# Moving the pools of small tiles so that large tiles begin at multiples of 64 bytes, in a hybrid GLA, retention and mixture-of-experts block

## The chip, the cores and the metric

The kernel runs on one core of one Trainium2 chip. The metric is the device time of the whole program in microseconds (us). Three runs of the kernel before gave 2324.79, 2324.49 and 2323.91 us; the median is 2324.49 us.

## What is computed

One decoder block over 1,024 tokens of width 1,024, all in float32. Cut to what matters:

```python
def reference(x, ...):
    u = _rmsnorm(x, norm_mix_w)
    proj = u @ w_in                               # 1024 x 11280: q, k, v, gates of two mixers
    o_gla = _gla_chunked(...)                     # 4 heads, gated linear attention
    o_ret = _retention_chunked(...)               # 4 heads, rotary, per-head decay
    y_a, y_b = o_gla @ w_branch_gla, o_ret @ w_branch_ret
    h = x + (sigmoid(mga) * y_a + sigmoid(mgb) * y_b) @ w_out
    t = _rmsnorm(h, norm_ffn_w)
    # router: best of 4 groups, then the 2 best of its 8 experts; 32 experts in all
    for each expert e, for the tokens that chose it:
        hid = silu(t @ wg[e]) * (t @ wu[e])       # 1024 -> 512
        ffn += weight * (hid @ wd[e])             # 512 -> 1024
    return _rmsnorm(h + ffn, norm_final_w)
```

## The kernel before, in words

**Products.** Nearly all of the arithmetic is done by one line, L153, in `Acc.add`. Each operand is split into two float32r parts, hi = the rounded value and lo = the rest (`split`, L136 to L143: ScalarE writes hi, VectorE writes lo), and a product is three matmuls into one PSUM bank: hi with hi, hi with lo, lo with hi. A matmul has a stationary operand (128 or 112 columns, loaded into the array) and a moving one (512 columns, that is 2,048 bytes of every partition). In the rows below the moving operand stands first behind the arrow: `bank<-w_hi,uh` moves `w_hi` over a stationary `uh`.

**First part, the mixers.** Two halves of 512 tokens. Weights come in slabs of 1 MB (`load_w`, L156): the SP queue loads `w_raw`, `split` makes `w_hi` and `w_lo`, one slab ahead of its use. Four kinds of products use them: `feat` (L320) has the weights stationary and moves `uh`/`ul`; `toks` (L328) has `uh`/`ul` stationary and moves the weights; `gla_y` and `ret_y` (L569, L761) have the weights stationary and move tiles of the pool `slots`; `project` (L806) has tiles of `slots` stationary and moves the weights. A fifth kind, in `ret_scores`, `ret_state` and `ret_out` (L650, L692, L721), has both operands in `slots`. The order of all steps is written out by hand in `prog` (L996 to L1127).

**Second part, the experts.** 32 experts, up to CAP = 112 rows each (L1173 to L1252). The rows are gathered by POOL's queue into `xg`, turned and split into `xh`/`xl` (L1184), which are the stationary operands of the gate and up products: eight blocks of 112 columns each, 448 bytes apart. The hidden layer is turned and split into `hh`/`hl` (L1230), four such blocks, stationary in the down products. The moving operands are the weights, `m_hi`/`m_lo`, split from `m_raw`: 6 slabs of 1 MB for each expert, 190 of them through whole raw buffers. A raw buffer (L1152) is one of eleven, used in turn: four of `upool`, two of `wraw`, five of `mraw`; for the last 58 slabs only the first six are used. The SP queue issues a slab's load as soon as VectorE has finished reading the buffer (L1199).

**Where tiles lie.** Pools are placed one behind the other in each partition in the order in which they are opened, and every tile takes a multiple of 32 bytes. `consts` begins at byte 16,512 and ends at 41,632. The memory map of the kernel before is then, by adding up the tiles:

| pool (opened in this order) | its large tiles | begins at byte | past a multiple of 64 |
|---|---|---|---|
| wraw | w_raw, m_raw | 41,632 | 32 |
| wsp | w_hi, w_lo, m_hi, m_lo | 58,016 | 32 |
| small (4,672 bytes) | none | 90,784 | 32 |
| ypool | yb, hid, hh, hl | 95,456 | 32 |
| rsm (3,680 bytes) | none | 111,840 | 32 |
| upool | uh, ul, m_raw | 115,520 | 0 |
| trig, slots (mixers) | slot | 148,288; 152,384 | 0 |
| mp, mk, mraw (experts, in the place of trig and slots) | xh, xl; xg; m_raw | 148,288; 163,264; 188,160 | 0 |

Of the kernel before, what the change touches and what calls it, by code (L numbers as in the profile page):

```python
# [18 lines left out]
F32 = mybir.dt.float32  # L19
F32R = mybir.dt.float32r  # L20
BF16 = mybir.dt.bfloat16
I32 = mybir.dt.int32
# [21 lines left out]
NEARLY = 2  # L44

# layout of the packed table of constants (columns)
# [9 lines left out]
def _const_table():  # L56
    """Constants that follow from the shapes alone."""
# [26 lines left out]
# 2*pi in three parts, the first two short enough for exact products  # L84
# [4 lines left out]
def hybrid_block(tc, a, out, dbg=None):  # L89
# [25 lines left out]
    psum = top.enter_context(tc.tile_pool(name="psum", bufs=8, space=bass.MemoryType.PSUM))  # L115
    wraw = top.enter_context(tc.tile_pool(name="wraw", bufs=2))
    wsp = top.enter_context(tc.tile_pool(name="wsp", bufs=2))
    small = top.enter_context(tc.tile_pool(name="small", bufs=2))
# [5 lines left out]
    def rsqrt(dst, src, n, p=128):  # L124
        """dst = 1/sqrt(src): a guess from the bits, then Newton's steps."""
        t = small.tile([128, 16], I32, name="rs_i", tag="rs_i")[:p, :n]
        y = small.tile([128, 16], F32, name="rs_y", tag="rs_y")[:p, :n]
        b = small.tile([128, 16], F32, name="rs_b", tag="rs_b")[:p, :n]
        DVE.tensor_scalar(t, src.bitcast(I32), 1, None, op0=OP.logical_shift_right)  # L129
        DVE.tensor_scalar(y.bitcast(I32), t, -1, 0x5f3759df, op0=OP.mult, op1=OP.add)  # L130
        for i in range(3):
            DVE.tensor_mul(b, y, y)  # L132
            DVE.scalar_tensor_tensor(b, b, -0.5, src, op0=OP.mult, op1=OP.mult)  # L133
            DVE.scalar_tensor_tensor(dst if i == 2 else y, b, 1.5, y, op0=OP.add, op1=OP.mult)

    def split(hi, lo, src, scale=None):  # L136
        """src (times scale per partition) = hi + lo, both with 12 significant bits."""
# [7 lines left out]
    class Acc:  # L145
        """Products of split operands summed in one bank."""
# [9 lines left out]
    def load_w(src, kt, n, swap=False):  # L156
        """A slab of weights [128, kt, n], split; swap: even columns first, then odd ones."""
# [18 lines left out]
    rsm = top.enter_context(tc.tile_pool(name="rsm", bufs=1))  # L176
# [3 lines left out]
    slots = mixers.enter_context(tc.tile_pool(name="slots", bufs=NSLOT))  # L180

# [48 lines left out]
    # kept across the halves  # L230
# [3 lines left out]
    # per assignment, for products with one-hots: its row in two parts, its weight in three  # L234
# [9 lines left out]
    junk = consts.tile([128, 512], BF16, name="junk")  # L244
# [5 lines left out]
    def sq_sum(dst, src, cols):  # L250
        """dst = sum of squares of src along its free axis."""
# [3 lines left out]
    def rms_tail(rstd, s2, n, p=128):  # L255
        """rstd[:, :n] = 1 / rms of n tiles' rows, from the squares of their column halves."""
# [5 lines left out]
    class Half:  # L262
        """One half of the sequence on its way through the mixers."""
# [16 lines left out]
        def norm_x(self, t):  # L280
            """The rows of one tile, scaled."""
# [19 lines left out]
        def start_x(self):  # L301
            """Tile after tile, as they come."""
# [17 lines left out]
        def feat(self, w, c0):  # L320
            """Features [c0, c0+128) of the slab w, for all tokens of the half: [128 features, 512]."""
# [6 lines left out]
        def toks(self, w, part, accs):  # L328
            """Rows 512*part.. of a [1024, 512] block of weights: adds to [128 tokens, 512] for each tile."""
# [24 lines left out]
        def decay_a(self):  # L354
            """log sigmoid(z) = min(z, 0) - ln(1 + exp(-|z|))"""
# [12 lines left out]
        def decay_b(self):  # L368
            self.mn = small.tile([128, 4], F32, name="mn")
# [8 lines left out]
        def decay_c(self):  # L378
            self.ep, self.en = [], []
            self.el = small.tile([128, 4, 4], F32, name="el")  # L380
# [8 lines left out]
            mn1 = small.tile([128, 1], F32, name="mn1")  # L389
# [3 lines left out]
        def decay_d(self):  # L393
            ps = bank()
            PE.transpose(ps[0:1, 0:128], self.mn1, ident)
            mn2 = small.tile([1, 2], F32, name="mn2")
# [60 lines left out]
        def gla_chunk(self, c, pair):  # L457
# [7 lines left out]
            for j in range(2):  # L465
# [5 lines left out]
                if not last:  # L471
# [5 lines left out]
                    else:  # L477
                        tmp = small.tile([128, 256], F32, name="s_tmp", tag="s_tmp")
# [4 lines left out]
        def gla_exact(self):  # L483
            """Where a chunk's decay leaves float32's range: the recurrence itself, one column of the
            state after the other, along the tokens."""
            half = self.half
            flag = nc.values_load(flag_i[0:1, half:half + 1], min_val=0, max_val=1)
            with tc.If(flag > 0):  # L488
                ones = small.tile([128, 1], F32, name="ones_f")
# [14 lines left out]
                for h in range(4):  # L504
# [10 lines left out]
                    with tc.For_i(0, 256, n) as i:  # L515
                        s0 = small.tile([128, n], F32, name="s0")
# [4 lines left out]
                        s1 = small.tile([128, n], F32, name="s1")  # L521
# [10 lines left out]
                        ob = small.tile([128, 4, n], F32, name="ob")  # L532
# [36 lines left out]
        def gla_y(self, w, c):  # L569
            """y_a, gated: features 256c.."""  # L570
# [46 lines left out]
        def rotary(self, w):  # L617
            """The slab's 256 features, rotated: raw and split, even ones then odd ones."""
# [31 lines left out]
        def ret_scores(self):  # L650
            """Scores, transposed, causal."""
            self.ph, self.pl = [], []
            for j in range(4):
# [11 lines left out]
                dg = small.tile([128, 128], F32, name="diag", tag="diag")  # L665
# [48 lines left out]
        def ret_hand(self):  # L714
            """What the rest of the head's work takes, kept apart from the next head's."""
# [5 lines left out]
        def ret_out(self, h):  # L721
            o = self.o
            mv = small.tile([128, 4, 2], F32, name="mv")
            for i in range(4):
# [10 lines left out]
                bs = small.tile([128, 6], F32, name="bs", tag="bs")  # L735
# [3 lines left out]
            # rstd of the decayed rows, with the decay: g^i / sqrt(g^2i var + eps)  # L739
# [101 lines left out]
        def route_a(self):  # L841
            """The rows that the experts gather."""
# [9 lines left out]
        def route_b(self):  # L852
# [11 lines left out]
            def first_max(src, n, name):  # L864
                """Its maximum along the last axis and the one-hot of the first place that has it."""
# [34 lines left out]
        def route_c(self):  # L900
            """Each assignment's place among its expert's rows."""
# [16 lines left out]
        def route_d(self):  # L918
            """The weights, in three parts of 8 bits for the products with one-hots."""
# [87 lines left out]
    def seq(z):  # L1007
        """Lists of steps of one half, by name."""
# [62 lines left out]
    def middle(half, mix):  # L1071
        """From the gated branch to the last head's projections; mix: steps put between, by place."""
# [70 lines left out]
    # =========================================================================  # L1143
# [1 line left out]
    moe = contextlib.ExitStack()  # L1145
    mp = moe.enter_context(tc.tile_pool(name="mp", bufs=2))
    mk = moe.enter_context(tc.tile_pool(name="mk", bufs=1))
    mraw = moe.enter_context(tc.tile_pool(name="mraw", bufs=NRAW))
# [24 lines left out]
    class Expert:  # L1173
        """One block of up to CAP rows of one expert."""
# [9 lines left out]
        def rows(self):  # L1184
            self.xh = mp.tile([128, 8, CAP], F32R, name="xh")
            self.xl = mp.tile([128, 8, CAP], F32R, name="xl")
# [27 lines left out]
        def room(self):  # L1214
            """For the hidden layer: rows, and turned in two parts."""
# [14 lines left out]
        def turn(self):  # L1230
# [4 lines left out]
            self.hh, self.hl = (z[:, :4 * CAP].rearrange("p (k t) -> p k t", k=4) for z in (self.hh, self.hl))  # L1235
# [26 lines left out]
    class Spill(Expert):  # L1262
        """The same with buffers that no load running ahead waits for, and the Pool's queue."""
# [4 lines left out]
        def room(self):  # L1268
            return [self.xg[:, :512], mp.tile([128, 8, CAP], F32R, name="hh", tag="xh").rearrange("p k t -> p (k t)"),
                    mp.tile([128, 8, CAP], F32R, name="hl", tag="xl").rearrange("p k t -> p (k t)")]  # L1270

    def overflow(xg):
        """The rows past the first CAP of an expert, a block of CAP at a time."""
        cf = mk.tile([1, 32], F32, name="cf")
        ci = mk.tile([1, 32], I32, name="ci")
        nb_f = mk.tile([1, 1], F32, name="nb_f")
        nb_i = mk.tile([1, 1], I32, name="nb_i")
# [5 lines left out]
        with tc.If(nb > 0):  # L1283
            gix2 = mp.tile([CAP, 32], I32, name="gix2")
            swt2 = mp.tile([CAP, 32], F32, name="swt2")
            with tc.For_i(0, nb, 1):
# [12 lines left out]
                with tc.For_i(0, NEXP, 1) as e:  # L1299
                    left = nc.values_load(ci[0:1, ds(e, 1)], min_val=0, max_val=SEQ)  # L1300
                    with tc.If(left > 0):
                        gi = mp.tile([CAP, 1], I32, name="gi")
                        wi = mp.tile([CAP, 1], F32, name="wi")
# [11 lines left out]
    # the down products of one come after the gate and up products of the next, save at a pause  # L1315
    pauses = (2, NEXP - 2, NEXP - 1)
    firsts = [mraw.tile([128, 2048], F32, name="m_raw", tag="m_raw") for i in range(NRAW)]
    for z in firsts[NEARLY:]:
        # the first rows come before these loads
# [83 lines left out]
```

## Time and profile before

| | |
|---|---|
| runs (three) | 2323.91 to 2324.79 us, median 2324.49 us |
| span of the profiled execution | 2320.6 us, from its first instruction to its last (3.9 us below the median of the runs; the page gives no other time of that execution) |
| busy, share of that span | PE 95%, weight loads 76%, VectorE 57%, ScalarE 47%, POOL 6% |
[...]
| DMA | 406 MB, 175 GB/s over the span |

How to read it: the mixers take the first two thirds of the span, with PE busy nearly throughout and the DMA engines about a third busy. After a thin stretch (end of the mixers, router) the experts follow, where PE and the DMA engines both show as full. Matmuls are pipelined, so that one lasts some 0.39 us and the next begins some 0.23 us after it; the distance between starts, not the duration, is the pace.

### The profile page before, as it was taken

To read this page: it belongs to the slowest core of one execution; us is meant where nothing else is said; L and a number is where in the kernel's file an instruction comes from. 1 tells how busy PE (TensorE), PEld (TensorE's weight loads), DVE (VectorE), ACT (ScalarE), POOL (GpSimd) and SP (SyncE) were. 2 spreads that over 40 slices of the span, in tenths; PEclk is the share of its full clock that TensorE was granted. 3 is DMA by queue.
4 is the path that set the end of the run, shared out by engine and by line. 5 is a ranking of instruction groups with operands and counts; after the bars stand their busy time and mean duration, and the time that the engine had idled before them with its cause. 6 is when DMAs were issued, how large, how long until landed. Compare 5 with 4: busy or idle time off the path is not lost. (4 is left out here: it accounts for less than half of the span.)

```text
span 2320.6 us, 25840 instructions
## 1 busy us (share of the span) xinstructions
PE 2214.0 (95%) x9950; PEld 1763.0 (76%) x9951; DVE 1313.6 (57%) x2015; ACT 1082.0 (47%) x1504; POOL 147.7 (6%) x116
## 2 busy tenths in 40 slices
PE   7999999999999999999999999999598999999993
PEld 5888788888888787887888888878476777777772
DVE  5523354525355627324435254536477888888886
ACT  5522333333233427323333332224276888888885
POOL 1000000000000011000000000001301111111102
PEclk9999999999999999999999999999799999999996
DMA  6422242222223544321532322229488999999995
GB/s 163 159 96 73 83 161 84 82 91 82 93 73 116 191 149 146 98 84 56 173 100 73 100 73 82 85 69 310 171 302 292 367 367 365 369 370 315 361 371 203
DMA packets 157953, 406.16 MB, mean 175 GB/s; under 512 B 13887, under 2 KB 65119, under 8 KB 133488
## 3 DMA queue, kind: packets, MB, share of 16 engines
q1 hardware_dynamic: 149088, 387.01, 47.4%
q0 software_dynamic: 8720, 17.28, 3.1%
q8 instruction: 83, 1.36, 0.2%
q14 instruction: 62, 0.51, 0.1%
HBM read 372.97 MB, written 44.04 MB: 180 GB/s over the span
## 5 line engine op out<-in xcount | busy, mean ns | idle before, releaser
L139 ACT CAST w_hi<-w_raw 128x1024 fp32r<-128x1024 f32 (+1 forms) x244 | 247.6, 1051 | 586.0 <-PE bank L153 510.2
L140 DVE TENSOR_TENSOR w_lo<-w_raw,w_hi 128x1024 fp32r<-128x1024 f32 (+1 forms) x244 | 291.7, 1218 | 379.0 <-ACT w_hi L139 358.9
L140 DVE TENSOR_TENSOR m_lo<-m_raw,m_hi 128x1024 fp32r<-128x1024 f32 x380 | 444.9, 1220 | 69.4 <-ACT m_hi L139 69.1
L139 ACT CAST m_hi<-m_raw 128x1024 fp32r<-128x1024 f32 x380 | 381.6, 1050 | 70.0 <-PE bank L153 65.7
L153 PE MATMUL bank<-w_hi,uh 128*128 128x512 f32 x768 | 305.0, 397 | 0.0
L153 PE MATMUL bank<-w_hi,ul 128*128 128x512 f32 x768 | 304.4, 396 | 0.0
L153 PE MATMUL bank<-w_lo,uh 128*128 128x512 f32 x768 | 302.1, 393 | 0.0
L153 PE MATMUL bank<-uh,w_hi 128*128 128x512 f32 x656 | 264.4, 403 | 8.1 <-ACTq L488 4.0
L153 PE MATMUL bank<-ul,w_hi 128*128 128x512 f32 x656 | 263.0, 401 | 0.0
L153 PE MATMUL bank<-uh,w_lo 128*128 128x512 f32 x656 | 262.9, 401 | 0.0
L153 PE MATMUL bank<-slot,w_hi 128*128 128x512 f32 x768 | 242.4, 397 | 1.1 <-DVE slot L143 0.8
L153 PE MATMUL bank<-m_lo,xh 128*112 128x512 f32 x512 | 207.8, 406 | 0.7 <-DVE m_lo L140 0.2
L153 PE MATMUL bank<-m_hi,xh 128*112 128x512 f32 x512 | 204.6, 400 | 3.1 <-ACT xh L139 2.9
L153 PE MATMUL bank<-m_hi,xl 128*112 128x512 f32 x512 | 203.0, 397 | 0.0
L153 PEld LDWEIGHTS bank<-slot,w_hi 128*128 128x128 f32 x768 | 144.4, 188 | 37.1 <-DVE slot L143 1.7
L153 PEld LDWEIGHTS bank<-w_hi,ul 128*128 128x128 f32 x768 | 144.2, 188 | 35.2
L153 PEld LDWEIGHTS bank<-w_lo,uh 128*128 128x128 f32 x768 | 144.2, 188 | 35.1
L153 PEld LDWEIGHTS bank<-w_hi,uh 128*128 128x128 f32 x768 | 144.3, 188 | 33.1
L153 PEld LDWEIGHTS bank<-uh,w_hi 128*128 128x128 f32 x656 | 125.5, 191 | 40.8 <-ACTq L488 4.3
L153 PE MATMUL bank<-slot,w_lo 128*128 128x512 f32 x384 | 151.7, 396 | 0.0
L153 PEld LDWEIGHTS bank<-uh,w_lo 128*128 128x128 f32 x656 | 125.3, 191 | 30.6
L153 PEld LDWEIGHTS bank<-ul,w_hi 128*128 128x128 f32 x656 | 125.5, 191 | 30.1
(264 smaller groups left out, 2893.7 us busy)
## 6 DMA issues: line engine op xcount, KB each, us to landing
w_raw<-in_w_in_dram SPq DMA_DIRECT2D x88, 1024.0 KB, 5.1
m_raw<-in_expert_w_down_dram SPq DMA_DIRECT2D x64, 1024.0 KB, 12.4
m_raw<-in_expert_w_gate_dram SPq DMA_DIRECT2D x63, 1024.0 KB, 12.6
m_raw<-in_expert_w_up_dram SPq DMA_DIRECT2D x63, 1024.0 KB, 12.4
w_raw<-in_w_branch_ret_dram SPq DMA_DIRECT2D x16, 1024.0 KB, 5.0
slot<-in_x_dram SPq DMA_DIRECT2D x32, 256.0 KB, 6.2
w_raw<-in_w_branch_gla_dram SPq DMA_DIRECT2D x8, 1024.0 KB, 5.2
w_raw<-in_w_out_dram SPq DMA_DIRECT2D x8, 1024.0 KB, 5.6
```

The lines of the kernel that those rows point to most:

```text
L139: ACT.copy(hi, src)
L140: DVE.tensor_sub(lo, src, hi.bitcast(F32))
L153: PE.matmul(self.ps, l, r, start=self.i == 0, stop=self.i == 3 * self.n - 1)
```

## The change

The pool `small` is split in three: what both parts of the kernel use stays in it (704 bytes), what only the mixers use goes to a new pool `mixs` that is opened behind `slots`, and what only the rarely used overflow path of the experts uses goes from `mk` and `mp` to a new pool `ov`, opened last. `small` and `rsm` are opened ahead of `wraw`; `mraw` and `mk` ahead of `mp`. The blocks of `xh`, `xl`, `hh` and `hl` lie 128 columns (512 bytes) apart and still hold 112. No instruction is added or removed, and no number of buffers changes. (The diff also drops comments, and gives `junk` a width of 512 + SPARE with SPARE = 0.)

```diff
+SPARE = 0
+ROW = 128
...
     psum = top.enter_context(tc.tile_pool(name="psum", bufs=8, space=bass.MemoryType.PSUM))
+    small = top.enter_context(tc.tile_pool(name="small", bufs=2))
+    rsm = top.enter_context(tc.tile_pool(name="rsm", bufs=1))
     wraw = top.enter_context(tc.tile_pool(name="wraw", bufs=2))
     wsp = top.enter_context(tc.tile_pool(name="wsp", bufs=2))
-    small = top.enter_context(tc.tile_pool(name="small", bufs=2))
...
     ypool = top.enter_context(tc.tile_pool(name="ypool", bufs=8))
-    rsm = top.enter_context(tc.tile_pool(name="rsm", bufs=1))
     upool = top.enter_context(tc.tile_pool(name="upool", bufs=4))
...
     slots = mixers.enter_context(tc.tile_pool(name="slots", bufs=NSLOT))
+    mixs = mixers.enter_context(tc.tile_pool(name="mixs", bufs=2))
...
-                        tmp = small.tile([128, 256], F32, name="s_tmp", tag="s_tmp")
+                        tmp = mixs.tile([128, 256], F32, name="s_tmp", tag="s_tmp")
...
     moe = contextlib.ExitStack()
+    mraw = moe.enter_context(tc.tile_pool(name="mraw", bufs=NRAW))
+    mk = moe.enter_context(tc.tile_pool(name="mk", bufs=1))
     mp = moe.enter_context(tc.tile_pool(name="mp", bufs=2))
-    mk = moe.enter_context(tc.tile_pool(name="mk", bufs=1))
-    mraw = moe.enter_context(tc.tile_pool(name="mraw", bufs=NRAW))
+    ov = moe.enter_context(tc.tile_pool(name="ov", bufs=1))
...
-            self.xh = mp.tile([128, 8, CAP], F32R, name="xh")
-            self.xl = mp.tile([128, 8, CAP], F32R, name="xl")
+            self.xh = mp.tile([128, 8, ROW], F32R, name="xh")[:, :, :CAP]
+            self.xl = mp.tile([128, 8, ROW], F32R, name="xl")[:, :, :CAP]
...
-            self.hh, self.hl = (z[:, :4 * CAP].rearrange("p (k t) -> p k t", k=4) for z in (self.hh, self.hl))
+            self.hh, self.hl = (z[:, :4 * ROW].rearrange("p (k t) -> p k t", k=4)[:, :, :CAP] for z in (self.hh, self.hl))
...
-            gix2 = mp.tile([CAP, 32], I32, name="gix2")
-            swt2 = mp.tile([CAP, 32], F32, name="swt2")
+            gix2 = ov.tile([CAP, 32], I32, name="gix2")
+            swt2 = ov.tile([CAP, 32], F32, name="swt2")
```

Ten more tiles go from `small` to `mixs` in the same way as `s_tmp` (`mn`, `el`, `mn1`, `mn2`, `diag`, `mv`, `bs`, and those of `gla_exact`), and six more from `mk` and `mp` to `ov`. Adding up the tiles as before, `small` now begins at 41,632, `rsm` at 42,336, and every large pool behind them at a multiple of 64: `wraw` at 46,016, `wsp` at 62,400, `ypool` at 95,168, `upool` at 111,552, `trig` and later `mraw` at 144,320, `slots` at 148,416, `mk` at 185,280, `mp` at 209,856.

## Rows read from the trace of the kernel before

**Rows 1.** Busy time by stretch: us, busy (x count) per engine, clock, DMA share, GB/s.
```profile
100.00:1500.00 1400.00, 1387.45 (x6206) 1126.88 (x6205) 628.12 (x1113) 473.78 (x714) 15.61 (x12) 0.99 0.31 103
1680.00:1685.00 5.00, 4.33 (x15) 3.38 (x16) 1.25 (x2) 1.06 (x2) 0.00 (x0) 0.55 0.63 190
1685.00:1765.00 80.00, 71.79 (x312) 53.02 (x311) 59.13 (x60) 56.38 (x67) 9.77 (x6) 0.95 0.84 293
1765.00:2130.00 365.00, 365.00 (x1681) 278.18 (x1681) 321.38 (x319) 297.51 (x359) 55.77 (x39) 1.00 0.99 354
2130.00:2275.00 145.00, 143.72 (x657) 108.32 (x656) 128.11 (x126) 119.48 (x142) 20.03 (x13) 1.00 0.98 354
```

**Rows 2.** PE in order of time, both operands in slots: start, us, instruction, count.
```profile
1227.24 12.41 PE L153 MATMUL bank<-slot 128*128 128x512 f32 x54
```

**Rows 3.** PE in order of time, weights moving (toks): first and last start of 96.
```profile
390.22 0.39 PE L153 MATMUL bank<-w_hi,uh 128*128 128x512 f32 x1
...
412.38 0.39 PE L153 MATMUL bank<-w_hi,ul 128*128 128x512 f32 x1
```

**Rows 4.** PE in order of time, weights stationary (feat): first and last start of 239.
```profile
81.75 0.40 PE L153 MATMUL bank<-ul,w_hi 128*128 128x512 f32 x1
...
137.50 0.40 PE L153 MATMUL bank<-uh,w_lo 128*128 128x512 f32 x1
```

**Rows 5.** PE in order of time, weights stationary, slots moving: first and last of 187.
```profile
1112.30 0.40 PE L153 MATMUL bank<-slot,w_lo 128*128 128x512 f32 x1
...
1155.87 0.40 PE L153 MATMUL bank<-slot,w_lo 128*128 128x512 f32 x1
```

**Rows 6.** PE in order of time, experts' gate and up products: first and last of 34.
```profile
1786.22 0.39 PE L153 MATMUL bank<-m_hi,xl 128*112 128x512 f32 x1
...
1793.86 0.40 PE L153 MATMUL bank<-m_hi,xl 128*112 128x512 f32 x1
```

**Rows 7.** PE in order of time, experts' down products: first and last of 30.
```profile
2253.35 0.39 PE L153 MATMUL bank<-m_hi,hl 128*112 128x512 f32 x1
...
2260.08 0.48 PE L153 MATMUL bank<-m_lo,hh 128*112 128x512 f32 x1
```

**Rows 8.** Groups of instructions, PE: busy us, mean ns of one, idle before.
```profile
L153 PE MATMUL bank<-w_hi,uh 128*128 128x512 f32 x768 | 305.0, 397 | 0.0
L153 PE MATMUL bank<-uh,w_lo 128*128 128x512 f32 x656 | 262.9, 401 | 0.0
L153 PE MATMUL bank<-slot,w_lo 128*128 128x512 f32 x384 | 151.7, 396 | 0.0
L153 PE MATMUL bank<-w_lo,slot 128*128 128x512 f32 x128 | 51.4, 402 | 0.0
```

**Rows 9.** Groups of instructions, VectorE: splits from w_raw and m_raw.
```profile
L140 DVE TENSOR_TENSOR w_lo<-w_raw,w_hi 128x1024 fp32r<-128x1024 f32 (+1 forms) x244 | 291.7, 1218 | 379.0 <-ACT w_hi L139 358.9 <-PE bank L644 8.6 <-PE bank L825 8.2
L140 DVE TENSOR_TENSOR m_lo<-m_raw,m_hi 128x1024 fp32r<-128x1024 f32 x380 | 444.9, 1220 | 69.4 <-ACT m_hi L139 69.1
```

**Rows 10.** Tile m_raw, us from a load's issue to landing, in 1765:1800, 2050:2080, 2130:2190.
```profile
DMA to landing us min/median/max: 5.0/6.9/8.9
...
DMA to landing us min/median/max: 22.5/23.1/24.2
...
DMA to landing us min/median/max: 10.3/12.4/13.6
```

**Rows 11.** Who waited for whom in 1800:2250: us in total, times, longest.
```profile
ACT m_hi L139 <- DMA m_raw<-in_expert_w_down_dram: 0.8, 1, 0.8
```

**Rows 12.** SP queue in order of time, end of the mixers: start, us, instruction, count.
```profile
1654.64 4.61 SPq L850 DMA_DIRECT2D u_d<-slot  x8
1661.66 2.00 SPq L1199 DMA_DIRECT2D m_raw<-in_expert_w_down_dram  x2
```

**Rows 13.** PE in order of time, the experts' first products at the lower clock.
```profile
1682.88 0.63 PE L153 MATMUL bank<-m_lo,xh 128*112 128x512 f32 x1
1683.31 0.63 PE L153 MATMUL bank<-m_hi,xl 128*112 128x512 f32 x1
```

More of the change, by code (lines that the diff above doesn't have):

```diff
@@ L243, in hybrid_block @@
     DVE.memset(base, 0.0)
-    junk = consts.tile([128, 512], BF16, name="junk")
+    junk = consts.tile([128, 512 + SPARE], BF16, name="junk")
     flag_i = consts.tile([1, 2], I32, name="flag_i")
@@ L368, in decay_b @@
         def decay_b(self):
-            self.mn = small.tile([128, 4], F32, name="mn")
+            self.mn = mixs.tile([128, 4], F32, name="mn")
             for h in range(4):
@@ L379, in decay_c @@
             self.ep, self.en = [], []
-            self.el = small.tile([128, 4, 4], F32, name="el")
+            self.el = mixs.tile([128, 4, 4], F32, name="el")
             for h in range(4):
@@ L388, in decay_c @@
                 self.en.append(n_)
-            mn1 = small.tile([128, 1], F32, name="mn1")
+            mn1 = mixs.tile([128, 1], F32, name="mn1")
             DVE.tensor_reduce(mn1, self.mn, axis=AX.X, op=OP.min)
@@ L395, in decay_d @@
             PE.transpose(ps[0:1, 0:128], self.mn1, ident)
-            mn2 = small.tile([1, 2], F32, name="mn2")
+            mn2 = mixs.tile([1, 2], F32, name="mn2")
             DVE.tensor_reduce(mn2[:, 0:1], ps[0:1, 0:128], axis=AX.X, op=OP.min)
@@ L488, in gla_exact @@
             with tc.If(flag > 0):
-                ones = small.tile([128, 1], F32, name="ones_f")
+                ones = mixs.tile([128, 1], F32, name="ones_f")
                 DVE.memset(ones, 1.0)
@@ L515, in gla_exact @@
                     with tc.For_i(0, 256, n) as i:
-                        s0 = small.tile([128, n], F32, name="s0")
+                        s0 = mixs.tile([128, n], F32, name="s0")
                         if half:
@@ L520, in gla_exact @@
                             DVE.memset(s0, 0.0)
-                        s1 = small.tile([128, n], F32, name="s1")
+                        s1 = mixs.tile([128, n], F32, name="s1")
                         ps = bank((128, 4, n))
@@ L531, in gla_exact @@
                                 PE.matmul(ps[:, t, u:u + 1], kv[:, 128 * t:128 * t + 128], ones, start=True, stop=True)
-                        ob = small.tile([128, 4, n], F32, name="ob")
+                        ob = mixs.tile([128, 4, n], F32, name="ob")
                         ACT.copy(ob, ps)
@@ L664, in ret_scores @@
                 hi, lo = slot(dt=F32R), slot(dt=F32R)
-                dg = small.tile([128, 128], F32, name="diag", tag="diag")
+                dg = mixs.tile([128, 128], F32, name="diag", tag="diag")
                 DVE.tensor_mul(dg, ps[:, :128], mask)
@@ L722, in ret_out @@
             o = self.o
-            mv = small.tile([128, 4, 2], F32, name="mv")
+            mv = mixs.tile([128, 4, 2], F32, name="mv")
             for i in range(4):
@@ L734, in ret_out @@
                     acc.add(o["ph"][j][:, s], o["pl"][j][:, s], o["vh"][j], o["vl"][j])
-                bs = small.tile([128, 6], F32, name="bs", tag="bs")
+                bs = mixs.tile([128, 6], F32, name="bs", tag="bs")
                 DVE.bn_stats(bs, ps)
@@ L1268, in room @@
         def room(self):
-            return [self.xg[:, :512], mp.tile([128, 8, CAP], F32R, name="hh", tag="xh").rearrange("p k t -> p (k t)"),
-                    mp.tile([128, 8, CAP], F32R, name="hl", tag="xl").rearrange("p k t -> p (k t)")]
+            return [self.xg[:, :512], mp.tile([128, 8, ROW], F32R, name="hh", tag="xh").rearrange("p k t -> p (k t)"),
+                    mp.tile([128, 8, ROW], F32R, name="hl", tag="xl").rearrange("p k t -> p (k t)")]
     def overflow(xg):
[L1274 to L1277, printed above, removed]
+        cf = ov.tile([1, 32], F32, name="cf")
+        ci = ov.tile([1, 32], I32, name="ci")
+        nb_f = ov.tile([1, 1], F32, name="nb_f")
+        nb_i = ov.tile([1, 1], I32, name="nb_i")
         DVE.tensor_reduce(nb_f, base[0:1, :], axis=AX.X, op=OP.max)
@@ L1301, in overflow @@
                     with tc.If(left > 0):
-                        gi = mp.tile([CAP, 1], I32, name="gi")
-                        wi = mp.tile([CAP, 1], F32, name="wi")
+                        gi = ov.tile([CAP, 1], I32, name="gi")
+                        wi = ov.tile([CAP, 1], F32, name="wi")
                         POOL.dma_start(gi, ix_d[:, ds(e, 1)])
```

## The prediction, made blind

> **What bounds the kernel now.** I read the stretches first. In the mixers, 100 to 1500 us, PE is busy 1387 of 1400 us while the DMA engines are 31% busy, and among the experts, 1765 to 2130 us, PE is busy all of the time [rows 1]. So PE's pace sets the time of both, and the pace is the distance between the starts of two matmuls, which I read next in order of time, in long rows without a break. [...] The reader is to see that they are not equally quick:
>
> - both operands in `slots`: 54 matmuls in 12.41 us; less the 0.39 us that the last one lasts, 53 distances of **226.8 ns** [rows 2];
> - weights moving over `uh`/`ul`: (412.38 - 390.22)/95 = **233.3 ns** [rows 3];
> - weights stationary, `uh`/`ul` moving: (137.50 - 81.75)/238 = **234.2 ns** [rows 4];
> - weights stationary, `slots` moving: (1155.87 - 1112.30)/186 = **234.2 ns** [rows 5];
> - experts, 112 stationary columns: 7.64/33 = **231.5 ns** for gate and up [rows 6], 6.73/29 = **232.1 ns** for down [rows 7].
>
> The memory map sorts them. `slots` begins at a multiple of 64 bytes and so do all its 2,048-byte tiles: both operands of [rows 2] are so placed. `wsp`, where every `w` and `m` operand lies, begins 32 bytes past one, and each of the other five rows has an operand there. It does not matter whether that operand moves [rows 3] or stands [rows 4, 5], and two such operands (`m` and `hh` [rows 7]) cost about what one does (`m` and `xh` [rows 6]). My reading: an operand 32 bytes past a multiple of 64 costs each of its matmuls 6.5 to 7.4 ns.
>
> Among the experts a second limit stands close behind. The DMA engines are 99% busy at 354 GB/s [rows 1], and a load of 1 MB takes 6.9 us from issue to landing around 1780 us but 23.1 us around 2065 us [rows 10]: transfers pile up by 16.2 us in 285 us, so DMA is 5.7% slower than PE asks for. 1,681 matmuls in 365 us [rows 1], 84 to an expert (72 products, 12 transposes), give PE's pace, 18.24 us an expert; DMA's is 18.24 x 1.057 = 19.3 us. The eleven raw buffers hide this with a lead won at the start, and the lead lasts just to the end: ScalarE waits for a slab once, 0.8 us [rows 11].
>
> **The change part by part.** No instruction is added, removed or put in another order; each keeps its queue.
>
> *Mixers.* `wsp` moves to 62,400 = 64 x 975, and all operands of L153 are then placed as those of [rows 2] are. I take 226.8 ns for all. The counts [rows 8]: 3 x 768 = 2,304 with weights moving over `uh`/`ul`, 6.5 ns each, 15.0 us; 3 x 656 = 1,968 `feat`, 7.4 ns, 14.6 us; `slot,w_lo` is one of three, so 3 x 384 = 1,152 at 7.4 ns, 8.5 us; `project`, 3 x 128 = 384, priced as [rows 3], 2.5 us. Together 40.6 us. PE is idle 0.9% of the stretch [rows 1] and a few matmuls start late for other reasons, so I count **39 us**. [...] I take 226.8 because it is the same instruction, shape and clock in the same part of the kernel.
>
> [...]
>
> *Experts.* There is no row with 112 aligned columns. [...] I take off the 6.5 ns that misplaced weights cost in [rows 3]: 225.0 ns, 72 x 6.5 = 0.47 us an expert, 15.0 us over 32. But most of it is not worth anything: PE at 17.77 us an expert outruns DMA at 19.3 us by 1.5 us each instead of 1.1. The lead is gone some seven experts sooner, and from there DMA sets the pace to the end. What remains is the head, about five experts up to 1780 us, where loads still land in 6.9 us and wait for a free buffer, and the tail, about four, where the last loads are issued and no further gathers follow: 9 x 0.47 = **4 us**. Bounds: 0 and 15.
>
> *Blocks 512 instead of 448 bytes apart.* 448 = 7 x 64, so the blocks of `xh` are at multiples of 64 already, and [rows 6, 7] differ by 0.6 ns though `hh` is 32 past one. I count nothing, between plus and minus 0.6 ns x 2,304 = 1.4 us. ScalarE and VectorE write them in rows of 112 with gaps; both have idle time among the experts (VectorE is busy 321 of 365 us [rows 1]), which hides it. Without that cover it would cost what their writes lengthen by, which no row prices.
>
> *Splits.* VectorE takes 1218 ns from `w_raw` (32 past) and 1220 ns from `m_raw`, most of whose buffers are at multiples of 64 [rows 9]: placement is worth nothing to it, and I count nothing. If PE gets faster, slabs must come sooner by 3%, against VectorE 45% busy in the mixers [rows 1].
>
> *New neighbours.* `mraw` now lies where `trig` and `slots` 0 to 17 were, so that a load into its second buffer waits for the slot from which the last normalised rows are stored. Those eight stores go out between 1654.6 and 1659.3 us, and the loads into `mraw` already follow at 1661.7 us in the same queue [rows 12]. A delay of one landing, 2 to 3 us, would stand before slabs seven and eight, whose turn at PE comes an expert later. Queued behind it on SP are only further loads. Nothing, at worst 3 us.
>
> [...]
>
> **Sum.** 39 + 4 = 43 us off the profiled execution's 2320.6 us, 2277.6 us; the median of the runs stands 3.9 us above that span, so **2281.5 us**.
>
> **Rivals.**
> 1. *The experts gain in full*: 40.6 + 15.0 = 56 us, **2269 us**. For it: PE never waits there now. Against: the growing time to landing [rows 10].
> 2. *Only the moving operand counts*, and stationary weights are slow for another reason (they are freshly written, say): 15.0 + 2.5 + 4 = 21.5 us, **2303 us**. Against: [rows 4, 5] agree to 0.1 ns with different moving tiles.
> 3. *The change does not do what it says*: what the matmuls at 231 ns and more share may be the pool `wsp`, not only its place; then nothing moves, **2324 us**. [...] Against it stand 54 and 96 matmuls in [rows 2, 3] with 6.5 ns between them and no other difference of form.
> [...]
>
> **How the numbers follow.** My forecast 0.66, rivals 0.12, 0.10, 0.08, 0.04. A measurement of this kernel can tell about 0.2%, 4.6 us, from no change. Faster: 0.66 + 0.12 + 0.10 = 0.88; same 0.08; slower 0.04. The forecast's own range is 2274 to 2289 (mixers 33 to 41, experts 0 to 8); to hold 8 in 10 with rival 1 below and rival 2 above I give 2267 to 2305.
>
> **What would show it.** Right: distances as in [rows 3 to 5] at 227 ns, [rows 6, 7] at 225; the experts begin 39 us sooner; time to landing rises faster than in [rows 10], and ScalarE's waits for `m_raw` loads grow from 0.8 us to tens of us in the last ten experts, with the clock at 1.00 or near. Wrong: distances still at 233 (rival 3), only [rows 3, 6] faster (rival 2), no waits for loads (rival 1), or a clock well under 0.9 after 2000 us (rival 4).

## The result, and the profile after

The changed kernel took 2286.78 us (median of 4 runs, 2282.20 to 2287.78) where the kernel before took 2324.2 us beside it: a ratio of 0.985, 95% interval 0.983 to 0.987, or 37 us less. The forecast was 2281.5 us, 43 us less. The profiled execution took 2287.78 us, its span is 2285.8 us; the comparison below is of spans, 2320.6 and 2285.8 us. Matmuls of `Acc.add` are at L156 now.

Busy time by stretch answers to [rows 1]: us, busy (x count) of PE, weight loads, VectorE, ScalarE and POOL, clock, DMA share, GB/s.

```profile
100.00:1500.00 1400.00, 1386.82 (x6346) 1154.78 (x6345) 639.85 (x1133) 481.41 (x726) 15.17 (x12) 0.99 0.31 104
1765.00:2130.00 365.00, 364.08 (x1678) 277.86 (x1677) 322.88 (x320) 299.04 (x360) 52.38 (x40) 1.00 1.00 358
2130.00:2275.00 145.00, 114.89 (x516) 85.12 (x514) 123.90 (x167) 109.86 (x150) 24.51 (x14) 0.91 0.88 316
```

In the mixers PE is busy as before, but gets through 6,346 matmuls and transposes where it got through 6,206: each is quicker. Among the experts it gets through 1,678 in 365 us, where it got through 1,681, so there is no gain. (The last stretch now holds the end of the program.)

PE in order of time, both operands in `slots`, then `toks`, `feat`, `slots` over weights (first and last of 96, 239 and 187), and the experts' gate and up products (first and last of 42); start, us, instruction. They answer to [rows 2 to 6].

```profile
1201.88 12.40 PE L156 MATMUL bank<-slot 128*128 128x512 f32 x54
...
1169.21 0.40 PE L156 MATMUL bank<-w_hi,uh 128*128 128x512 f32 x1
...
1190.77 0.39 PE L156 MATMUL bank<-w_hi,ul 128*128 128x512 f32 x1
...
80.35 0.40 PE L156 MATMUL bank<-ul,w_hi 128*128 128x512 f32 x1
...
134.33 0.39 PE L156 MATMUL bank<-uh,w_lo 128*128 128x512 f32 x1
...
1090.31 0.39 PE L156 MATMUL bank<-slot,w_lo 128*128 128x512 f32 x1
...
1132.49 0.39 PE L156 MATMUL bank<-slot,w_lo 128*128 128x512 f32 x1
...
1728.11 0.40 PE L156 MATMUL bank<-m_hi,xh 128*112 128x512 f32 x1
...
1737.52 0.40 PE L156 MATMUL bank<-m_hi,xl 128*112 128x512 f32 x1
```

That is 226.7, 227.0, 226.8, 226.8 and 229.5 ns from start to start. Over all such distances of the trace (those under 260 ns) the mixers' products stand at 226.8 to 226.9 ns, the experts' at 230.6 (gate and up, 231.5 before) and 230.1 (down, 231.9 before).

The groups of PE [rows 8] and VectorE's splits [rows 9], out<-in xcount | busy us, mean ns of one:

```profile
L156 PE MATMUL bank<-w_hi,uh 128*128 128x512 f32 x768 | 300.7, 392 | 0.0
L156 PE MATMUL bank<-uh,w_lo 128*128 128x512 f32 x656 | 259.0, 395 | 0.0
L156 PE MATMUL bank<-slot,w_lo 128*128 128x512 f32 x384 | 149.1, 390 | 0.0
L156 PE MATMUL bank<-w_lo,slot 128*128 128x512 f32 x128 | 50.8, 397 | 0.0
...
L143 DVE TENSOR_TENSOR w_lo<-w_raw,w_hi 128x1024 fp32r<-128x1024 f32 (+1 forms) x244 | 291.7, 1218 | 360.8 <-ACT w_hi L142 342.4
L143 DVE TENSOR_TENSOR m_lo<-m_raw,m_hi 128x1024 fp32r<-128x1024 f32 x380 | 445.2, 1219 | 72.5 <-ACT m_hi L142 72.1
```

One matmul is 5 to 6 ns shorter as well; the splits kept their length. The weight loads (188 ns for `uh` beneath `w_hi`) kept theirs.

**Where the time came from.** First and last product of the experts, kernel before, then after:

```profile
1682.32 0.77 PE L153 MATMUL bank<-m_hi,xh 128*112 128x512 f32 x1
...
2282.18 0.40 PE L153 MATMUL bank<-m_hi,hl 128*112 128x512 f32 x1
```

```profile
1646.97 0.77 PE L156 MATMUL bank<-m_hi,xh 128*112 128x512 f32 x1
...
2247.56 0.39 PE L156 MATMUL bank<-m_hi,hl 128*112 128x512 f32 x1
```

The experts begin 35.3 us sooner, take 600.6 us where they took 599.9, and 38.2 us follow where 38.4 did: 35.3 - 0.7 + 0.2 = 34.8 us, the difference of the spans. All of it is the mixers'.

Their quicker distances are worth 40.8 us by the trace (2,304 x 6.5, 1,968 x 7.4, 1,152 x 7.5, 384 x 6.5 and, in `slots`, 480 x 0.7 ns). Some 5 us of that went at the router of the first half, where PE pauses 3.4 us (3.1 us in the kernel before) and the granted clock then falls, to 0.50 of full speed at the lowest; there matmuls stand 0.43 us apart (879.43 to 881.56 us, as in [rows 13]). The windows from that pause on, after and before:

```profile
865.00:885.00 20.00, 16.64 (x67) 14.55 (x65) 17.36 (x37) 11.88 (x19) 8.02 (x6) 0.66 0.35 131
```

```profile
887.00:907.00 20.00, 16.95 (x85) 14.12 (x83) 19.14 (x54) 13.60 (x22) 9.22 (x8) 0.91 0.51 177
```

At 0.66 and 0.91 of full speed, 20 us differ by 5.0 us of work. (In the changed kernel it is 0.50 from 870 to 880 us. Over the whole span the clock is 0.978 before and 0.976 after.) The other stretches at 0.50 nearly cancel: up to the experts' first product the two traces have 65.6 us of them after and 55.8 us before, which is 4.9 us of work. How long the clock stays down around the router differs from one profiled execution to the next (13.7 us in this trace, 6.8 us in that of again, which is the same kernel): in the kernels below whose mixers run at 226.9 ns the experts begin at 1639.8 to 1648.3 us, those with halved loads apart.

**Among the experts**, from a load's issue to its landing, in 1730:1765, 2015:2045 and 2095:2155 [rows 10], and ScalarE's waits for loads, 1800:2250 (us, times, longest) [rows 11]:

```profile
DMA to landing us min/median/max: 4.9/7.9/10.9
...
DMA to landing us min/median/max: 23.9/25.6/26.0
...
DMA to landing us min/median/max: 13.8/14.9/16.3
```

```profile
ACT m_hi L142 <- DMA m_raw<-in_expert_w_down_dram: 5.5, 8, 1.2
...
ACT m_hi L142 <- DMA m_raw<-in_expert_w_up_dram: 1.6, 3, 0.6
...
ACT m_hi L142 <- DMA m_raw<-in_expert_w_gate_dram: 0.2, 1, 0.2
```

The waits grew from 0.8 [rows 11] to 7.3 us: the lead of the loads is now used up before the end.

### The profile page after: what moved, and what is told of

Read it like the earlier page. It is cut to its first block, busy times and chain, and to the rows that moved or that the text cites. A ratio compares the mean times of both kernels' runs of the same rounds, so it can differ in the third digit from the quotient of the medians.

```text
span 2285.8 us, 25815 instructions
## 1 busy us (share of the span) xinstructions
PE 2177.7 (95%) x9950; PEld 1765.8 (77%) x9951; DVE 1312.4 (57%) x2015; ACT 1083.5 (47%) x1504; POOL 140.9 (6%) x116
## 2 busy tenths in 40 slices
DMA packets 157953, 406.16 MB, mean 178 GB/s; under 512 B 13887, under 2 KB 65119, under 8 KB 133488
## 5 line engine op out<-in xcount | busy, mean ns | idle before, releaser
L143 DVE TENSOR_TENSOR w_lo<-w_raw,w_hi 128x1024 fp32r<-128x1024 f32 (+1 forms) x244 | 291.7, 1218 | 360.8 <-ACT w_hi L142 342.4
L143 DVE TENSOR_TENSOR m_lo<-m_raw,m_hi 128x1024 fp32r<-128x1024 f32 x380 | 445.2, 1219 | 72.5 <-ACT m_hi L142 72.1
L156 PE MATMUL bank<-w_hi,uh 128*128 128x512 f32 x768 | 300.7, 392 | 0.0
L156 PE MATMUL bank<-w_lo,uh 128*128 128x512 f32 x768 | 299.3, 390 | 0.0
L156 PE MATMUL bank<-w_hi,ul 128*128 128x512 f32 x768 | 299.3, 390 | 0.0
L156 PE MATMUL bank<-uh,w_hi 128*128 128x512 f32 x656 | 261.0, 398 | 8.2 <-PEq L491 8.0
L156 PE MATMUL bank<-ul,w_hi 128*128 128x512 f32 x656 | 259.4, 395 | 0.0
L156 PE MATMUL bank<-uh,w_lo 128*128 128x512 f32 x656 | 259.0, 395 | 0.0
L156 PE MATMUL bank<-slot,w_hi 128*128 128x512 f32 x768 | 237.0, 390 | 1.1 <-DVE slot L146 0.8
L156 PE MATMUL bank<-m_lo,xh 128*112 128x512 f32 x512 | 207.5, 405 | 1.0 <-DVE m_lo L143 0.3
L156 PE MATMUL bank<-m_hi,xh 128*112 128x512 f32 x512 | 204.6, 400 | 2.0 <-ACT xh L142 1.6
L156 PE MATMUL bank<-m_hi,xl 128*112 128x512 f32 x512 | 202.7, 396 | 0.0
L156 PEld LDWEIGHTS bank<-slot,w_hi 128*128 128x128 f32 x768 | 144.0, 188 | 32.0 <-DVE slot L146 1.7
L156 PEld LDWEIGHTS bank<-w_hi,ul 128*128 128x128 f32 x768 | 144.2, 188 | 30.0
L156 PEld LDWEIGHTS bank<-w_lo,uh 128*128 128x128 f32 x768 | 144.3, 188 | 29.4
L156 PEld LDWEIGHTS bank<-w_hi,uh 128*128 128x128 f32 x768 | 144.3, 188 | 29.4
L156 PEld LDWEIGHTS bank<-uh,w_hi 128*128 128x128 f32 x656 | 125.5, 191 | 36.7 <-ACTq L491 4.5
L156 PE MATMUL bank<-slot,w_lo 128*128 128x512 f32 x384 | 149.1, 390 | 0.0
L156 PEld LDWEIGHTS bank<-uh,w_lo 128*128 128x128 f32 x656 | 125.2, 191 | 26.4
L156 PEld LDWEIGHTS bank<-ul,w_hi 128*128 128x128 f32 x656 | 125.6, 191 | 25.7
```

Source lines behind the costliest of these rows:

```text
L143: DVE.tensor_sub(lo, src, hi.bitcast(F32))
L156: PE.matmul(self.ps, l, r, start=self.i == 0, stop=self.i == 3 * self.n - 1)
```

## The experiments

Twelve kernels, each the changed kernel with the edit shown, but for the one that starts from the kernel before. The table has for each how far its `uh`/`ul` and its `slots` lie from `wsp`, in bytes modulo 512; mean distances from start to start in ns, for weights over `uh`, `uh` over weights, `slots` over weights and the experts' gate and up products; the us from the first to the last expert product; and the time with the 95% interval of its ratio to the kernel before. In all but cap128 and the two with halved loads each engine has the same instructions in the same order as in the kernel that they start from, but for the clearing of a pad.

| kernel | uh, slots from w | w,uh | uh,w | slot,w | m,x | experts | median us | ratio (95%) |
|---|---|---|---|---|---|---|---|---|
| before (profiled) | 160, 160 | 233.3 | 234.2 | 234.2 | 231.5 | 599.9 | | |
| again | 0, 0 | 226.9 | 226.9 | 226.8 | 230.5 | 598.3 | 2285.3 | 0.984 to 0.988 |
| spare16 | 0, 0 | 226.9 | 226.9 | 226.8 | 230.3 | 602.3 | 2283.5 | 0.982 to 0.986 |
| spare32 | 0, 0 | 226.9 | 226.8 | 226.8 | 230.0 | 596.8 | 2282.4 | 0.982 to 0.985 |
| row112 | 0, 0 | 226.9 | 226.9 | 226.8 | 232.0 | 599.8 | 2281.7 | 0.982 to 0.986 |
| pad32 | 32, 32 | 233.3 | 233.3 | 233.3 | 233.2 | 603.1 | 2323.5 | 0.9995 to 1.002 |
| slotvar | 64, all | 233.3 | 229.1 | 232.1 | 231.6 | 601.7 | 2312.9 | 0.995 to 0.998 |
| cap128 | 0, 0 | 226.9 | 226.9 | 226.8 | 228.3 | 598.8 | 2284.8 | 0.983 to 0.986 |
| ndeep198 | 0, 0 | 226.9 | 226.9 | 226.8 | 230.3 | 594.9 | 2283.3 | 0.982 to 0.985 |
| before352 | 0, 0 | 226.9 | 226.9 | 226.8 | 231.8 | 599.5 | 2282.0 | 0.982 to 0.986 |
| pad128 | 128, 256 | 232.8 | 232.9 | 227.0 | 231.5 | 599.1 | 2303.5 | 0.992 to 0.996 |
| half | 0, 0 | 226.9 | 226.9 | 226.8 | 230.2 | 601.3 | 2286.5 | 0.983 to 0.987 |
| half_pad32 | 32, 32 | 233.3 | 233.3 | 233.3 | 233.2 | 606.7 | 2321.5 | 0.999 to 1.002 |

### The changed kernel once more (again)

> The changed kernel once more, as the base for the three others: 2287 us (2282 to 2288), distances between matmul starts of 226.9 ns in the mixers and 230.6 (gate and up) and 230.0 ns (down) among the experts. It tells how far its own spread (2282.2 to 2287.8 us so far) goes.

2285.3 us (2280.6 to 2291.7), with the distances expected. The base for the rest; differences under some 4 us are not told apart from it.

### Everything 32 bytes past a multiple of 64 (spare16)

```diff
-SPARE = 0
+SPARE = 16
```

> Everything of the change stays (order of the pools, blocks 512 bytes apart), but junk is 32 bytes wider, so that wraw, wsp, ypool, upool, slots and the experts' pools all begin 32 bytes past a multiple of 64. Theory A, the place of an operand, and one misplaced operand costs what two do: 233.3 to 234.2 ns in all products of the mixers, those with both operands in slots too (480 of 512 columns, which the kernel before ran at 227), experts back to 231.5; 2287 + 39 + 480 x 7 ns = about 2326 to 2332 us, no faster than the kernel before. Theory B, each misplaced operand costs its own 7 ns: 240 ns, since now both are misplaced; some 2365 us. Rival C, the order of the pools (new neighbours, no small tiles between the large ones) made the gain: distances stay at 227, 2287 us.

Theories A and B both fell: not a nanosecond came back. Groups of PE in this kernel:

```profile
L156 PE MATMUL bank<-w_hi,uh 128*128 128x512 f32 x768 | 300.3, 391 | 0.0
L156 PE MATMUL bank<-uh,w_lo 128*128 128x512 f32 x656 | 258.8, 394 | 0.0
L156 PE MATMUL bank<-slot,w_lo 128*128 128x512 f32 x384 | 148.9, 389 | 0.0
L156 PE MATMUL bank<-slot 128*128 128x512 f32 x480 | 114.0, 393 | 3.1 <-ACT slot L142 3.1
```

So an operand's place modulo 64 is not what costs. Either the order of the pools made the gain (C), or the distance between two operands' places: all pools are shifted alike here. The memory map of the kernel before allows the second: from `wsp` (58,016) to `upool` (115,520) are 57,504 bytes, 112 x 512 + 160, and to `slots` 184 x 512 + 160; in the changed kernel 96 x 512 and 168 x 512, without a rest. Two `slots` always were whole multiples of 512 apart, and these ran well in both kernels.

### All large tiles at multiples of 512 (spare32)

```diff
-SPARE = 0
+SPARE = 32
```

> junk is 64 bytes wider, so that all large tiles begin at multiples of 512 bytes (and of 256) and not at 448 past one. Theory A, for TensorE a multiple of 64 is enough: 226.9 and 230.6 ns as in the changed kernel. Rival B, TensorE gains from a larger multiple too: under 226. For the transfers, theory C, the trace so far: place makes no difference, slabs 36 to 132 land within 310 to 313 us, 2287 us. [...]

A and C held. From the landing of slab 36 to that of slab 132 went 309.5 us, against 310.9 and 313.0 us in the two profiles of the changed kernel and 309.9 us before; from issue to landing, 2015:2045:

```profile
DMA to landing us min/median/max: 24.1/24.8/25.4
```

The runs show no gain of the loads by their place: of the kernels whose loads still go to places off a multiple of 512, spare16 took 310.0 us and before352 309.0 us for the same 96 slabs, and the medians from issue to landing in this window lie on both sides of 24.8 us (25.6 us in the changed kernel, 24.6 us in row112).

### Blocks 448 bytes apart again (row112)

```diff
-ROW = 128
+ROW = 112
```

> The changed kernel's places, with the blocks of xh, xl, hh and hl 448 bytes apart as before. Theory A, spacing is worth nothing (448 is a multiple of 64): 230.6 and 230.0 ns, 2287 us. Rival B, the 0.9 to 1.8 ns that the experts' distances did gain came from the spacing and the place of the weights is worth nothing with 112 columns: 231.5 ns as in the kernel before; since the transfers bind there, the time is 2287 to 2289 us all the same.

B for the distances: 232.0 and 232.2 ns (down), as slow as before. What the experts' products did gain came from the 512 bytes between blocks, which let every block lie a multiple of 512 from the weights. The time does not show it, as both theories said.

### 32 bytes between wsp and the rest (pad32)

```diff
+    pad = top.enter_context(tc.tile_pool(name="pad", bufs=1))
+    DVE.memset(pad.tile([128, PAD], F32, name="pad"), 0.0)
     ypool = top.enter_context(tc.tile_pool(name="ypool", bufs=8))
```

with PAD = 8.

> A tile of 32 bytes stands between wsp and ypool, and all else is as in the changed kernel: w and m operands at multiples of 64 as there, everything that meets them (uh, ul, slots, xh, hh) 32 past one. Theory R (formed after everything 32 past a multiple of 64 ran as fast as the changed kernel): what costs is the distance between the moving and the stationary operand's places, and any 32 bytes between them cost: 233 to 234 ns where w meets uh or slots, 227 with both in slots, about 2287 + 39 = 2322 to 2326 us. Rival C, the order of the pools made the gain (it is kept here): 227 everywhere, 2283 to 2287 us. The experts, by R, stay at 230 to 232 ns and bound by the transfers.

R, to the nanosecond, and C is out: the order of the pools is the changed kernel's, `w` lies at the changed kernel's place, and the gain is gone.

```profile
L157 PE MATMUL bank<-w_hi,uh 128*128 128x512 f32 x768 | 305.1, 397 | 0.0
L157 PE MATMUL bank<-uh,w_lo 128*128 128x512 f32 x656 | 263.1, 401 | 0.0
L157 PE MATMUL bank<-slot,w_lo 128*128 128x512 f32 x384 | 151.2, 395 | 0.0
L157 PE MATMUL bank<-slot 128*128 128x512 f32 x480 | 114.0, 393 | 3.1 <-ACT slot L143 3.1
```

The first three are as long as before [rows 8], within 1 ns; the last, with both operands in `slots`, kept its 393 ns of the changed kernel.

### Every distance at once (slotvar)

```diff
-        return slots.tile(list(shape), dt, name="slot", tag="slot")
+        z = slots.tile([shape[0], 512 + STEP], dt, name="slot", tag="slot")[:, :512]
+        return z if len(shape) == 2 else z.rearrange("p (a b) -> p a b", a=shape[1])
```

with STEP = 8, and the pad above with PAD = 16.

> The tiles of slots lie 2080 instead of 2048 bytes apart, so that the distance between a slot and the w operand or the other slot it meets takes every multiple of 32 bytes; a pad of 64 bytes stands between wsp and ypool, so that uh and ul lie 64 bytes further from w (modulo 512). Theory R with 64 bytes as its period: products of slots at even multiples of 32 at 227, at odd ones at 233 to 234; uh and ul at 227; half of the 2016 products with slots lose 7 ns, 2283 + 7 = about 2291 us. Theory R with a longer period (128, 256 or 512): products at 64 bytes cost too, so that uh and ul run at 229 to 235 ns and the slots' distances have a pattern of that period; 4272 products with uh and ul and most of 2016 with slots, 2 to 7 ns each, 2295 to 2325 us. Rival C, the order of the pools: 227 everywhere, 2283 to 2287 us.

A period of 64 is out: 64 bytes apart, `w` over `uh` takes 233.3 ns and `uh` over `w` 229.1.

```profile
L158 PE MATMUL bank<-w_hi,uh 128*128 128x512 f32 x768 | 304.6, 397 | 0.0
L158 PE MATMUL bank<-uh,w_lo 128*128 128x512 f32 x656 | 260.6, 397 | 0.0
```

The products with `slots` were meant to show the pattern and did not: those of `slots` over weights take 230 to 234 ns at every distance, even the 48 at a distance of 0 (231.0 ns). Each stands between others of other distances, and the neighbours' operands may count too, which these runs do not show; no pair of operands whose distance I sorted by explained more than a quarter of the spread in `slots` over weights. That part is inconclusive.

### The kernel before with one pad (before352)

```diff
     wsp = top.enter_context(tc.tile_pool(name="wsp", bufs=2))
+    pad = top.enter_context(tc.tile_pool(name="pad", bufs=1))
+    DVE.memset(pad.tile([128, 88], F32, name="pad"), 0.0)
     small = top.enter_context(tc.tile_pool(name="small", bufs=2))
...
-            gix2 = mp.tile([CAP, 32], I32, name="gix2")
-            swt2 = mp.tile([CAP, 32], F32, name="swt2")
+            gix2 = mk.tile([CAP, 32], I32, name="gix2")
+            swt2 = mk.tile([CAP, 32], F32, name="swt2")
```

> The kernel before, its pools in their old order, its blocks 448 bytes apart and its large tiles still 32 bytes past a multiple of 64 in wraw and wsp; only a pad of 352 bytes stands behind wsp (and two small tiles of the overflow path move from mp to mk to make room for it). With it upool, slots and mp lie a whole multiple of 512 bytes from wsp, where they lay 160 past one. Theory R, the distance between the places of the two operands decides: 226.8 ns in all products of the mixers, 39 us less than before, 2280 to 2286 us. Rival C, the order of the pools: 233 to 234 ns, 2320 us as before. My first reading, an operand 32 bytes past a multiple of 64 costs: w still is, and now uh and slots are too, 233 to 234 ns, 2320 to 2326 us.

R again: 2282.0 us. One pad gives all that the change gave, with the old order of pools and every large tile of `wsp`, `upool` and `slots` 32 bytes past a multiple of 64.

```profile
L155 PE MATMUL bank<-w_hi,uh 128*128 128x512 f32 x768 | 300.4, 391 | 0.0
L155 PE MATMUL bank<-uh,w_lo 128*128 128x512 f32 x656 | 258.9, 395 | 0.0
L155 PE MATMUL bank<-slot,w_lo 128*128 128x512 f32 x384 | 149.0, 389 | 0.0
```

### 128 and 256 bytes (pad128)

The pad of pad32 with PAD = 32, and a second one of 128 bytes ahead of `trig`.

> The changed kernel with a pad of 128 bytes between wsp and ypool and another of 128 between upool and the mixers' pools: uh and ul lie 128 bytes past a multiple of 512 from w, the slots 256 past one. It asks which multiple the distance has to be. Period 64 is out already (w over uh at 64 took 233.3 ns). Period 128: 226.9 ns everywhere, 2281 to 2287 us. Period 256: 229 to 234 ns with uh and ul, 227 with slots, 4272 products x 2 to 7 ns, 2292 to 2315 us. Period 512 or more: 229 to 234 ns in both, 2296 to 2324 us.

This is what a period of 256 would give: 128 bytes cost nearly as much as 32 did, 256 nothing. In this kernel every large tile of `wsp`, `upool` and `slots` begins at a multiple of 64, as the change wanted it, and it is still some 18 us slower than the changed kernel.

```profile
L156 PE MATMUL bank<-w_hi,uh 128*128 128x512 f32 x768 | 304.4, 396 | 0.0
L156 PE MATMUL bank<-uh,w_lo 128*128 128x512 f32 x656 | 262.0, 399 | 0.0
L156 PE MATMUL bank<-slot,w_lo 128*128 128x512 f32 x384 | 148.9, 389 | 0.0
```

The experts' blocks of 448 bytes, which meet the weights at every multiple of 64, agree only loosely. In row112 and before352 alike, the distance from the start before to their own is shortest for blocks that lie 256 from the weights (229.1 and 229.0 ns) and longest for those at 128 (234.2 and 233.9), but 231 to 232 ns for those at 0. Taken to the next start instead, it is 231.3 and 231.1 ns at 256, 234.1 and 233.8 at 128, 232.2 and 231.5 at 0.

### 128 columns for the experts (cap128)

```diff
-CAP = 112
+CAP = 128
```

> CAP is 128: the experts' stationary blocks have 128 columns, without gaps. Theory A, 112 columns are what keeps the experts at 230 ns: 226.9 ns there, as in the mixers. Rival B, it is the traffic of the splits and transfers beside them: 230 ns still. In both the transfers bind (the gathers and scatters grow by a seventh, 2 x 2 MB, some 6 us at 354 GB/s, and come on top), so the time is 2285 to 2297 us.

Between the two: gate and up at 228.3 ns (230.6 with 112 columns), down at 230.2 as in the changed kernel (230.1). What is left in gate and up stands mostly at the first blocks: up to 2080 us, the products of the fifth to seventh of the eight blocks follow each other at 227 ns, as A has it, and those of the first block at 233; the changed kernel has 230 and 232 there. (From 2091 us on some steps stand elsewhere in this program.)

```profile
L156 PE MATMUL bank<-m_lo,xh 128*128 128x512 f32 x512 | 205.4, 401 | 0.8 <-DVE m_lo L143 0.2
L156 PE MATMUL bank<-m_hi,hl 128*128 128x512 f32 x256 | 100.1, 393 | 0.2 <-DVE hl L143 0.2
```

### Halved loads, at both distances (half, half_pad32)

```diff
-            SP.dma_start(raw, src)
+            n = shape[1] // 2
+            SP.dma_start(raw[:, :n], src[:, :n])
...
-            split(hi[:, s], lo[:, s], raw[:, s])
+            split(hi[:, s], lo[:, s], raw[:, :n])
```

> Left out: the second half of every expert slab's load (0.5 MB for 1 MB; both halves of the split read the first half). Everything else as in the changed kernel. The transfers then no longer bind among the experts. From the first to the last expert product the kernels so far took 597 to 603 us, the one before 600. Theory A, waits for loads cost the changed kernel only what its last ten experts show, and the pace of 230 ns is that of 112 columns and the splits: 230 ns still, 592 to 597 us from first to last product, 2275 to 2281 us in all. Rival B, the loads' traffic in SBUF slows the matmuls: 227 to 228 ns, another 5 to 8 us less, 2267 to 2275 us.

> The same halved loads, with the 32 bytes of pad between wsp and ypool that made the mixers run at 233.3 ns and the experts at 233.2 ns. Beside the run with halved loads alone it shows what the distance is worth among the experts where transfers do not bind. Theory A: 233.2 ns against 230.5, times 2304 products, 6 us more from first to last product (598 to 603 us), and 39 us more in the mixers: 2318 to 2326 us. Rival B, the experts' time is set by something else than the pace of the products (splits, the hand-over between slabs): the same time from first to last product within 2 us as the other run, only the 39 us of the mixers.

These two leave out half of every expert slab's load, so that they compute something else. Some steps stand elsewhere in them; at the end ScalarE begins the final norm ahead of the last hidden layer, which adds a wait of PE. The first with halved loads, a stretch of the experts:

```profile
1770.00:2140.00 370.00, 370.00 (x1713) 283.42 (x1712) 329.32 (x326) 304.82 (x367) 58.33 (x41) 1.00 0.69 196
```

Its time from issue to landing in 2015:2045:

```profile
DMA to landing us min/median/max: 3.5/4.1/4.8
```

And that wait of PE's, in us:

```profile
PE bank L1239 <- DVE hid L1233: 7.0, 1, 7.0
```

In the changed kernel the same wait is:

```profile
PE bank L1238 <- DVE hid L1232: 0.8, 1, 0.8
```

Less these 6.2 us, 601.3 are 595.1 us from first to last product, as A has it. The whole time, 2286.5 us, is above what either theory said: that wait is in it, and in the profiled execution the experts begin at 1655.1 us, 8.2 us later than in the changed kernel, with 80.2 us at a granted clock of 0.50 up to there instead of 65.6. With the DMA engines 69% busy and no load issued from 1700 us on landing later than 6.3 us, the distance is still 230.2 ns (A), and an expert takes 18.16 us (mean of the sixth to the twentieth), 18.19 in the changed kernel, 18.24 before. With 32 bytes of pad it takes 18.31 us, and all of them together 5.4 us more (A said 6). So PE sets the experts' pace nearly throughout, and taking away half of the loads' traffic quickens it by no more than 0.03 us an expert.

### Eleven buffers to the end (ndeep198)

```diff
-NDEEP = 132
+NDEEP = 198
```

> NDEEP is 198: the loads use all eleven raw buffers to the end, instead of six from slab 132 on. Theory A, the change to six buffers leaves the DMA engines short of work where PE has no lead any more (DMA 91% busy from 2050 to 2100 us, slab 132 issued 2036, slab 138 only 2066 us): without it DMA stays full, slab 189 lands 3 to 5 us sooner, 2279 to 2284 us where the changed kernel has 2283 to 2287. Rival B, the DMA engines are full on the whole and the loss is made up elsewhere, or the final loads of h, which then use the eleven buffers in turn too, come later: 2283 to 2290 us.

The window 2050:2100, this kernel, then the changed one:

```profile
2050.00:2100.00 50.00, 49.95 (x233) 38.03 (x232) 44.73 (x46) 40.98 (x51) 7.76 (x5) 1.00 1.01 359
```

```profile
2050.00:2100.00 50.00, 49.42 (x230) 37.56 (x229) 43.52 (x45) 40.27 (x50) 6.45 (x5) 1.00 0.91 313
```

The gap of the DMA engines is gone, ScalarE waits 0.8 us for loads instead of 7.3, and the experts take 594.9 us, the least of all. In the time it cannot be told from the changed kernel (2283.3 us), and neither can spare32, row112 or before352. None is shown to beat it. Both theories allow this time.

## Why the prediction came out, point by point

- **The number was right, its reason was not.** The step that failed is "My reading: an operand 32 bytes past a multiple of 64 costs each of its matmuls 6.5 to 7.4 ns". spare16 and before352 have such operands throughout the mixers and lose nothing; pad32 moves them 32 bytes apart and loses all; pad128 has every one at a multiple of 64 and loses half. What costs in the mixers is that the moving and the stationary operand are not a multiple of 256 or 512 bytes apart: 226.8 to 227.0 ns in the table's rows where they are, 229.1 to 234.2 where they are not or, as with the `slots` of slotvar, not always. No rival of mine had this. [rows 2 to 5] could not separate the two: wherever one operand was misplaced, the two were also 160 bytes apart. The map showed that, had I taken differences; and "two such operands cost about what one does" was a hint at it. That the sum came out is luck: the pools that the change leaves between `wsp`, `upool` and `slots` happen to be multiples of 512 bytes long, so that a move meant for 64 brought every distance to 0, the distance of [rows 2], from which the 226.8 ns were taken.
- **226.8 ns for all products of the mixers**: 226.8 to 226.9. **39 us**: 40.8 us by the distances, of which 35.3 us arrived in the profiled execution, the clock at the first half's router taking some 5.
- **Experts at 225.0 ns, 4 us**: wrong in size. Measured 230.6 and 230.1 ns and no gain (599.9 to 600.6 us). The 6.5 ns were taken over from 128 columns and from operands 160 bytes apart; the experts' blocks lay at all distances from 0 to 480 bytes. With 128 columns gate and up gain 2.3 ns and down nothing; a rest of 1.5 and 3.4 ns over the mixers' pace remains, in gate and up mostly at the first blocks. An expert took 18.19 us where I had 17.77. What it did gain, 0.05 us each, is less than the 6.5 us of added waits for loads.
- **Blocks 512 bytes apart, nothing**: wrong in principle, 1.4 to 2.1 ns a product (row112), though the time does not show it.
- **DMA binds soon behind PE** (rival 1 out): the waits for loads grew as forecast, but to 7.3 us and not to tens, since PE hardly got quicker. (96 slabs, 16 experts' worth, landed in 313.0 us, 19.6 us an expert where I had 19.3.) **Splits, new neighbours: nothing**: 1218 and 1219 ns; the first loads into `mraw` went out at 1626.7 us, 35.0 sooner [rows 12], as all else.
- **Rival 2** is out ([rows 4, 5] gained as [rows 3] did), **rival 3** by the time. **Rival 4**, a clock well under 0.9 after 2000 us: it stayed at 1.00 among the experts until 2130 us.

Why the distance matters is not shown. The weight load for one matmul (188 ns) runs while the one before is under way (in the changed kernel a load from 1170.37 us, a matmul from 1170.37 to 1170.76 us); that the two collide there is a guess that no run tests. What the runs show is the size: 32 bytes between the two operands took 233.3 ns, none 226.9.

## What to carry to other kernels

When equal matmuls run at two paces, compare the places of their two operands with each other, not only with a round number: here a pad of 352 bytes, which puts them a multiple of 512 apart, was worth 37 us. A change that moves everything at once can be right for a reason that is not its own; shift everything together once, and one thing alone once, before believing the reason.

## What I had not expected of the hardware

- In the mixers' float32r matmuls of 512 columns, 32 bytes between the places of the two operands (modulo 512) cost 6.4 ns of 227; 64 cost that or 2.3 ns, by which of the two moves; 128 cost 6; 256, measured with `slots` alone, nothing.
- 112 stationary columns took longer than 128: 230.6 against 228.3 ns in gate and up (not in down).
- With 128 rows an expert's loads came quicker: slabs 36 to 132 landed within 304.4 us, instead of 306.7 to 313.0 in the other kernels with whole loads. The gathers did not grow as I had expected (406.18 MB moved in all, 406.16 in the changed kernel). I have no cause for it.
